# Attention by pairs of heads: scores in two row tiles, weights divided by their sums only in the output, keys tiled from the first meta token

## The chip, the core and the metric

The kernel runs on one core of a Trainium2 chip. TensorE (PE) multiplies matrices out of the on-chip memory SBUF into the accumulators in PSUM; PEld is its loading of the stationary operand. VectorE (DVE), ScalarE (ACT) and GpSimd (POOL) do elementwise work, and SyncE (SP) issues most of the DMAs. Every engine works through its own list of instructions in the order written. The metric is the time of one execution in microseconds, as the median of several runs.

## The reference, cut to what matters

Sixteen learned meta tokens go ahead of 512 tokens of width 1024. Layer 0 is an attention with a forget gate, layer 1 a gated recurrence, and each is followed by a mixture of 32 experts. The change is in layer 0's attention, with 16 heads of width 64:

```
h = concatenate([meta, x], axis=1)                 # 16 + 512 = 528 places
q, k = rms_norm per head (both with gains);  v;  log_f = log_sigmoid(f_logit + b_f)
cum = cumsum(log_f, axis=1)
s = einsum('bhqd,bhkd->bhqk', qi, kh) * scale + cum_q - cum_k
p = softmax(where(key_pos <= q_pos, s, -1e30), axis=-1)
o = einsum('bhqk,bhkd->bhqd', p, vh)
h = h + o @ w_out
```

All of it is float32.

## The kernel before

`fox` first projects tokens to q, k and v, half a matrix at a time (`chunk`), then calls `attend`. The projections split every float32 operand in a rounded part (`hi`) and its remainder (`lo`) and add three products. The query tokens lie in four tiles of 128 (`NT = 4`); the meta tokens are kept apart: `vm` holds the values of the 16 meta places and `v[:, j]` those of token tile j. Query tile i sees n = 16 + 128(i+1) keys: 144, 272, 400 and 528.

`attend` walks over the 16 heads. For a head,

- `key_bias` loads -cum of the keys, the same row on all 128 partitions, by four DMAs into one of four buffers `bias`, and POOL adds the causal mask to the four diagonal blocks;
- `scores` multiplies q and k. A head has 64 rows, head a = 0 of a pair on partitions 0 to 63 and a = 1 on 64 to 127. Each of the four blocks is three products of hi and lo (the first pair of heads: one product in float32). Then DVE adds bias to the scores, writes them over the bias and takes the row maximum in one instruction per block (line 703), and forms the exponent's offset `nb`;
- `soften` is ACT's exponential in place with the row sum `sm`, four instructions;
- `normalise` is DVE's multiplication of the weights by 1/`sm`, four instructions (line 724);
- `turn` transposes the weights on PE, 14 blocks (first 16 meta keys of each query tile, then 128 keys at a time), through two PSUM buffers `ptp`, each copied out by ACT or DVE to `PTm` and `PT`;
- `mix`, once per pair, multiplies the transposed weights with the values into `po`, the two heads side by side in two column tiles of 64, and `K.a.put` splits `po` into `ahi` and `alo` for the output projection.

The order is written by hand in the loop at the end of `attend`: the turn of head t-2, the softmax of head t-1 and the mix of an older pair are slipped between the four score blocks of head t, so that PE always has something else to do. `meta_scores` and `meta_turn` do the 16 meta queries of all heads. After the attention, `out_project` begins with ACT's split of a weight (`whi`, line 278), and opens the room for the experts' weights, which are then streamed from HBM.

Of the kernel before, what the change touches and what calls it, by code (L numbers as in the profile page):

```python
# [20 lines left out]
D = 1024  # L21
# [141 lines left out]
class Normed:  # L163
# [3 lines left out]
    def __init__(self, K, src, gain, pool, wk, ps, ptag, rs=None):  # L167

        self.K, self.src, self.wk, self.ps, self.ptag, self.rs = K, src, wk, ps, ptag, rs
        self.gb = gain[:, :, None]  # L170
        self.xs = {}
        self.hi = pool.tile([128, KJ, S], FR, name="xhi")
        self.lo = pool.tile([128, KJ, S], FR, name="xlo")

        self.m = pool.tile([128, KJ, 2 * M], FT, name="xm")
        K.nc.gpsimd.memset(self.m, 0.0)

    def tokens(self, i, j):
        cs = slice(128 * i, 128 * i + 128)
        return self.hi[:, j, cs], self.lo[:, j, cs]  # L180
# [31 lines left out]
    def turn(self, i, xs):  # L212
# [3 lines left out]
        for j0 in range(0, KJ, 4):  # L216
# [4 lines left out]
            if i == NT:  # L221
                nc.vector.tensor_tensor(self.m[:, j0:j0 + 4, :M], p[:, :, :r], g, op=OP.mult)
                continue
# [3 lines left out]
        cs = slice(128 * i, 128 * i + 128)  # L227
        for js, t in ts:
            nc.scalar.activation(self.hi[:, js, cs], t, AF.Copy)  # L229
        for js, t in ts:  # L230
            nc.vector.tensor_tensor(self.lo[:, js, cs], t, self.hi[:, js, cs].bitcast(FT), op=OP.subtract)  # L231

# [79 lines left out]
def row_terms(x, W, i, late=False):  # L312

    xs = [x.tokens(i, j) for j in range(KJ)]
# [12 lines left out]
def project(K, x, W, i, p, between, late):  # L327

    ts = row_terms(x, W, i, late)
# [36 lines left out]
def fox(K):  # L366
# [3 lines left out]
    with tc.tile_pool(name="ax", bufs=1, reuse_waits="tile") as per:  # L370
# [3 lines left out]
        vm = per.tile([M, D], FT, name="vm")  # L374
# [11 lines left out]
        with tc.tile_pool(name="ap", bufs=1, reuse_waits="tile") as mid, \  # L386
# [8 lines left out]
            def load(i):  # L395
                if i == NT:

                    nc.sync.dma_start(vm, K.meta_tokens)
                    loaded[i] = vm, M
                    return  # L400
# [3 lines left out]
            x = Normed(K, loaded.pop, gain, mid, nw, ps, "tr")  # L404
# [34 lines left out]
            def meta_done(mr, kind, half):  # L439
                if kind == "v":  # L440
                    mr.sum(vm[:, 512 * half:512 * half + 512])
                    return
# [5 lines left out]
            def meta_product(n):  # L448
                return MetaRows(K, x.m[:, :, :M], ps.tile([128, 512], FT, name="pm", tag="pm"), n)

            def chunk(kind, half, nxt):
# [3 lines left out]
                for i in range(NT):  # L455
# [9 lines left out]
                    project(K, x, W2, i, p, between, early)  # L465
                    if i == 0 and early:
                        mr = meta_product(2 * KJ)
# [8 lines left out]
                    if nxt and mr is None and not turns:  # L476
                        mr = meta_product(KJ)
# [83 lines left out]
        attend(K, qT, kT, v, vm, cq)  # L561


def forget_gate(K, x, wf, mid, ps, later, cq):
# [10 lines left out]
    def logits():  # L575
        p = ps.tile([128, 512], FT, name="pf", tag="pm")
        ts = []
        for j in range(KJ):
            ts += parts((wh[:, j], wl[:, j]), (x.hi[:, j], x.lo[:, j]))
# [44 lines left out]
def attend(K, qT, kT, v, vm, cq):  # L624
    nc, tc = K.nc, K.tc
    with tc.tile_pool(name="at", bufs=1, reuse_waits="tile") as mid, \
            tc.tile_pool(name="au", bufs=3, reuse_waits="tile") as wk, \
            tc.tile_pool(name="av", bufs=1, space=PSUM, reuse_waits="tile") as ps:
        B = K.B + [mid.tile([128, TOT], FT, name=f"bias{n}") for n in range(2, 4)]
        bias, PT, QK = {}, {}, {}  # L630

        def prepare(hd):
            bias[hd] = B[hd % 4]
            key_bias(K, hd, B[hd % 4])

# [28 lines left out]
        def split(hp):  # L664

            QK[hp] = []
            for n, src in (("q", qT[:, hp, M:]), ("k", kT[:, hp])):
                hi, lo = [wk.tile([128, src.shape[1]], FR, name=n + m, bufs=2) for m in ("hi", "lo")]
# [4 lines left out]
        def scores(hd):  # L673

            a, hp = hd % 2, hd // 2
            r = slice(64 * a, 64 * a + 64)

            qk = [(q[r], k[r]) for q, k in (parts(*QK[hp]) if hp else [(qT[:, 0, M:], kT[:, 0])])]
            b = bias[hd]
            mx = wk.tile([128, NT], FT, name="mx")  # L680
            nb = wk.tile([128, NT], FT, name="nb")
            todo = []
            for i in range(NT):
                n = M + 128 * (i + 1)
                qi = slice(128 * i, 128 * i + 128)
                bi = b[:, OFF[i]:OFF[i] + n]
                if i == 0:
                    pb = ps.tile([128, 512], FT, name="s0", tag="s0")
                if i < 2:
                    p = pb[:, 144 * i:144 * i + n]  # L690
                    accumulate(nc, p, [(q[:, qi], k[:, :n]) for q, k in qk])
                elif i == 2:
                    p = ps.tile([128, 512], FT, name="s2", tag="s2")[:, :n]
                    accumulate(nc, p, [(q[:, qi], k[:, :n]) for q, k in qk])
                else:
                    p = ps.tile([128, 2, 512], FT, name="s3", tag="s3")[:, :, :n // 2]
                    for u in range(2):
                        accumulate(nc, p[:, u], [(q[:, qi], k[:, n // 2 * u:n // 2 * (u + 1)]) for q, k in qk])
                    bi = bi.rearrange("q (u c) -> q u c", u=2)
                todo.append((p, bi))  # L700
                yield
            for i, (p, bi) in enumerate(todo):
                nc.vector.tensor_tensor_reduce(bi, p, bi, 1.0, NEG, op0=OP.add, op1=OP.max, accum_out=mx[:, i:i + 1])
            cqh = cq[:, :NT, hd]
            nc.vector.tensor_tensor(mx, mx, cqh, op=OP.add)
            nc.vector.tensor_tensor(nb, cqh, mx, op=OP.subtract)
            held[hd] = nb
            if a == 0 and hp + 1 < NH // 2:
                split(hp + 1)

        def soften(hd, nb):
            b = bias[hd]
            sm = wk.tile([128, NT], FT, name="sm")
            for i in range(NT):
                bi = b[:, OFF[i]:OFF[i] + M + 128 * (i + 1)]
                nc.scalar.activation(bi, bi, AF.Exp, bias=nb[:, i:i + 1], accum_out=sm[:, i:i + 1])
            return sm

        def normalise(hd, sm):
            b = bias[hd]  # L720
            nc.vector.reciprocal(sm, sm)
            for i in range(NT):
                bi = b[:, OFF[i]:OFF[i] + M + 128 * (i + 1)]
                nc.vector.tensor_scalar(bi, bi, sm[:, i:i + 1], None, op0=OP.mult)

        def turn(hd):

            b = bias.pop(hd)
            pt = wk.tile([128, 1280], FT, name="PT", bufs=4)
            ptm = wk.tile([M, S], FT, name="PTm", bufs=4)  # L730
            PT[hd] = (pt, ptm)
            for j in range(-1, NT):
                p = ps.tile([128, 512], FT, name="ptp", tag="pt", bufs=2)
                for i in range(max(j, 0), NT):
                    o = OFF[i] + (M + 128 * j if j >= 0 else 0)
                    n = 128 if j >= 0 else M
                    nc.tensor.transpose(p[:n, 128 * i:128 * i + 128], b[:, o:o + n], K.ident)  # L737
                c = 128 * max(j, 0)
                if j < 0:
                    nc.scalar.activation(ptm, p[:M], AF.Copy)  # L740
                elif j % 2:
                    nc.vector.tensor_copy(pt[:, POFF[j]:POFF[j] + S - c], p[:, c:])
# [1295 lines left out]
```

## Time and profile before

| | us |
|---|---|
| time, median of 3 runs (1782.38 to 1784.61) | 1783.42 |
| time of the profiled execution | 1778.16 |
| its span in the profile | 1776.2 |
| PE busy | 1621.1 |
| DVE busy | 773.2 |
| ACT busy | 411.7 |

Busy times are shares of the whole span. Matmuls are pipelined, so that one matmul's duration holds some latency, and what one costs in a stream is read from the start of one to the start of the next. The attention is about 116 us of the span, from 207 to 323 us.

### The profile page before, as it was taken

To read this page: it belongs to the slowest core of one execution; us is meant where nothing else is said; L and a number is where in the kernel's file an instruction comes from. 1 tells how busy PE (TensorE), PEld (TensorE's weight loads), DVE (VectorE), ACT (ScalarE), POOL (GpSimd) and SP (SyncE) were. 2 spreads that over 40 slices of the span, in tenths; PEclk is the share of its full clock that TensorE was granted. 3 is DMA by queue.
4 is the path that set the end of the run, shared out by engine and by line. 5 is a ranking of instruction groups with operands and counts; after the bars stand their busy time and mean duration, and the time that the engine had idled before them with its cause. 6 is when DMAs were issued, how large, how long until landed. Compare 5 with 4: busy or idle time off the path is not lost.

```text
span 1776.2 us, 23560 instructions
## 1 busy us (share of the span) xinstructions
PE 1621.1 (91%) x9397; PEld 881.2 (50%) x9397; DVE 773.2 (44%) x1834; ACT 411.7 (23%) x867; POOL 241.7 (14%) x205
## 2 busy tenths in 40 slices
PE   5998999986999999999979989989779999999997
PEld 3666766553344443433346667767533433333333
DVE  5664388353234342333461545665513333232334
ACT  5433266341001000000043323334401000000000
POOL 1412344100000000000032222313000000000000
PEclk9999899996999999999989999999889999999999
DMA  4212554448999999999911211114689999999995
GB/s 169 77 63 80 137 105 81 167 150 324 419 419 419 419 419 419 420 419 419 376 59 39 94 48 49 54 50 184 252 329 419 419 419 419 419 419 419 420 420 213
DMA packets 103558, 472.73 MB, mean 266 GB/s; under 512 B 16224, under 2 KB 34704, under 8 KB 54800
## 3 DMA queue, kind: packets, MB, share of 16 engines
q1 hardware_dynamic: 97248, 458.12, 65.8%
q0 software_dynamic: 5008, 8.76, 1.5%
q10 hardware_dynamic: 1184, 4.26, 0.6%
q8 instruction: 76, 1.25, 0.3%
q14 instruction: 42, 0.34, 0.1%
HBM read 472.97 MB, written 6.39 MB: 270 GB/s over the span
## 4 chain that ended last, share of the span: by engine, by line
PE 48%; DMA 35%; DVE 10%; ACT 4%; issue 1%; POOL 0%; ACTq 0%; DVEq 0%; SPq 0%; POOLq 0%
DMA w<-in_moe_w_up_dram 23%; PE pp L888 12%; DMA w<-in_moe_w_down_dram 11%; PE pa L1610 10%; PE pp L331 5%; PE py L1610 4%; PE pc L304 2%; PE s L304 2%; PE ptp L737 2%; PE pm L348 1%; PE po L761 1%; DVE Q L1066 1%; ACT xs L210 1%; PE pt L1591 1%; PE po L304 1%
## 5 line engine op out<-in xcount | busy, mean ns | idle before, releaser
L1610 PE MATMUL pa<-w,hm 128*64 128x512 f32 x1024 | 237.0, 600 | 16.9 <-DMA w<-in_moe_w_up_dram 16.9
L1610 PE MATMUL py<-w,hT 128*64 128x512 f32 x1024 | 244.6, 597 | 0.6 <-DMA w<-in_moe_w_down_dram 0.6
L1610 PE MATMUL pa<-w,xT 128*64 128x512 f32 x1024 | 234.5, 598 | 8.8 <-DMA w<-in_moe_w_up_dram 8.8
L286 POOL TENSOR_TENSOR wlo<-w,whi 128x2048 fp32r<-128x2048 f32 (+1 forms) x27 | 120.9, 4480 | 384.9 <-ACT whi L278 367.7
L1661 DVE TENSOR_TENSOR h<-pc,h 128x512 f32<-128x512 f32 x256 | 159.1, 682 | 21.3 <-PE pc L304 21.3
L1610 PEld LDWEIGHTS pa<-w,hm 128*64 128x64 f32 x1024 | 75.9, 138 | 169.3 <-issue 130.7
L1610 PEld LDWEIGHTS pa<-w,xT 128*64 128x64 f32 x1024 | 78.8, 137 | 156.4 <-issue 130.7
L1610 PEld LDWEIGHTS py<-w,hT 128*64 128x64 f32 x1024 | 73.7, 136 | 154.5 <-issue 137.8
L1596 DVE TENSOR_TENSOR hm<-pt,mg 128x512 f32<-128x512 f32 x32 | 22.1, 691 | 288.9 <-PE pt L1591 288.9
L1408 POOL DMA_INDIRECT xg<-xd,row x32 | 32.1, 1003 | 850.1 <-PE pt L1591 698.2
L1596 DVE TENSOR_TENSOR xT<-pt,mg 128x512 f32<-128x512 f32 x32 | 22.1, 691 | 284.7 <-PE pt L1591 284.7
L304 PE MATMUL pc<-yhi,OT 128*128 128x512 f32 (+1 forms) x288 | 127.4, 442 | 3.6 <-DVE OT L1644 2.9
L1625 ACT ACTIVATE sg<-pa 128x512 f32<-128x512 f32 x32 | 19.1, 597 | 463.3 <-PE pa L1610 463.3
L304 PE MATMUL pc<-ylo,OT 128*128 128x512 f32 (+1 forms) x288 | 114.8, 399 | 1.1 <-DVE ylo L1651 0.8
L1638 ACT ACTIVATE hT<-pth 128x512 f32<-128x512 f32 x32 | 19.2, 599 | 331.8 <-PE pth L1636 331.8
L331 PE MATMUL pp<-whi,xlo 128*128 128x512 f32 x192 | 80.2, 417 | 2.5 <-DVE xlo L231 2.5
L331 PE MATMUL pp<-whi,xhi 128*128 128x512 f32 x192 | 79.6, 415 | 2.1 <-ACT xhi L229 2.1
L304 PEld LDWEIGHTS pc<-yhi,OT 128*128 128x128 f32 (+1 forms) x288 | 52.9, 184 | 40.8 <-DVE h L1661 24.8
L888 PE MATMUL pp<-xhi,whi 128*128 128x512 f32 x168 | 71.9, 428 | 0.0
L888 PE MATMUL pp<-xlo,whi 128*128 128x512 f32 x168 | 67.9, 404 | 0.0
L278 ACT ACTIVATE whi<-w 128x2048 fp32r<-128x2048 f32 x32 | 61.1, 1917 | 0.0
L1650 ACT ACTIVATE yhi<-py,slot 128x512 fp32r<-128x512 f32 x64 | 42.2, 685 | 73.2 <-PE pc L304 46.7
(396 smaller groups left out, 2426.8 us busy)
## 6 DMA issues: line engine op xcount, KB each, us to landing
w<-in_moe_w_up_dram SPq DMA_DIRECT2D x256, 1024.0 KB, 19.9
w<-in_moe_w_down_dram SPq DMA_DIRECT2D x124, 1024.0 KB, 20.5
w<-in_hg_w_in_dram SPq DMA_DIRECT2D x16, 1024.0 KB, 5.3
w<-in_fox_w_in_dram SPq DMA_DIRECT2D x12, 1024.0 KB, 5.3
bias<-ncum SPq DMA_DIRECT2D x16, 264.0 KB, 4.1
w<-in_fox_w_out_dram SPq DMA_DIRECT2D x4, 1024.0 KB, 5.1
xd<-xn ACTq DMA_DIRECT2D x8, 512.0 KB, 4.9
w<-in_moe_w_down_dram SPq DMA_DIRECT2D x8, 512.0 KB, 16.8
```

The source lines that it names most:

```text
L278: nc.scalar.activation(hi, raw, AF.Copy)
L286: e.tensor_tensor(lo[:, js], raw[:, js], hi[:, js].bitcast(FT), op=OP.subtract)
L304: nc.tensor.matmul(p, a, b, start=(n == 0), stop=(n == len(terms) - 1))
L331: K.nc.tensor.matmul(p, a, b, start=(n == 0), stop=(n == len(ts) - 1))
L737: nc.tensor.transpose(p[:n, 128 * i:128 * i + 128], b[:, o:o + n], K.ident)
L888: nc.tensor.matmul(p, a, b, start=(m == 0), stop=(m == len(terms) - 1))
L1408: K.nc.gpsimd.indirect_dma_start(x, None, K.xd[self.layer], bass.IndirectOffsetOnAxis(ap=row, axis=0), bounds_check=K.xd[self.layer].shape ...
L1596: nc.vector.tensor_tensor(xT[:, js], p[:, :, :n], gain[:, js, None].to_broadcast([128, 4, n]), op=OP.mult)
L1610: nc.tensor.matmul(p[c][64 * a:64 * a + 64], x[:, j, 64 * a:64 * a + 64], w[a][c], start=(j == 0), stop=(j == nj - 1), skip_group_check=Tr ...
L1638: nc.scalar.activation(hT[:, :, :n], pt[:, :, :n], AF.Copy)
L1650: nc.scalar.activation(hi[:n], py[:n], AF.Copy, scale=g)
L1661: nc.vector.tensor_tensor(h[:, cs], p[:r], h[:, cs], op=OP.add)
```

## The change

It changes five things in layer 0's attention.

1. Values are projected for places and not for tokens: `v[:, 0]` now begins with the 16 meta places, and `vl` holds the last 16 places. For this the normalised tokens lie behind the meta tokens in one array (`lead`).
2. Keys are tiled from the first meta place, so that tile j holds places 128j to 128j+127, and each query tile has one further edge of 16 keys, which only its last 16 queries see. The turn copies four small blocks (`PTe`, 16 keys by 16 queries) where it copied 16 keys by 512 queries (`PTm`), and `mix` has eight products of 16 columns for a pair where it had two of 512.
3. `scores` does a pair of heads at a time, the two heads' matmuls in turn, each into a PSUM bank of its own. The 528 keys are two blocks of 264.
4. `normalise` is gone. The weights are turned undivided; 1/`sm` of a pair is spread over 64 partitions per head by eight small matmuls with the identity (`pr`), copied by ACT (`on`), and multiplied to `po` by DVE on the way out.
5. The loop runs over 8 pairs and two steps more: scores of pair t and mix of pair t-2 in pieces by turns, then the whole turn of pair t-1, then the exponentials of pair t. There are five bias buffers, and the double buffering of small tiles goes from 3 to 2.

```diff
-    def __init__(self, K, src, gain, pool, wk, ps, ptag, rs=None):
+    def __init__(self, K, src, gain, pool, wk, ps, ptag, rs=None, lead=0):
...
-        self.hi = pool.tile([128, KJ, S], FR, name="xhi")
-        self.lo = pool.tile([128, KJ, S], FR, name="xlo")
+        self.hi = pool.tile([128, KJ, lead + S], FR, name="xhi")
+        self.lo = pool.tile([128, KJ, lead + S], FR, name="xlo")
...
+        def scores(hp):
...
+            for n, blocks in enumerate((((0, 0, 0, 144), (1, 144, 0, 272)), ((2, 0, 0, 400),), ((3, 0, 0, 264),),
+                                        ((3, 0, 264, 264),))):
+                p = ps.tile([128, 2, 512], FT, name="s", tag="s", bufs=2)
+                for i, c, k0, w in blocks:
+                    for t, (q, k) in enumerate(qk):
+                        for a in range(2):
+                            r = slice(64 * a, 64 * a + 64)
+                            nc.tensor.matmul(p[:, a, c:c + w], q[r, 128 * i:128 * i + 128], k[r, k0:k0 + w],
+                                             start=(t == 0), stop=(t == len(qk) - 1))
+                for a in range(2):
...
+                        nc.vector.tensor_tensor_reduce(bi, p[:, a, c:c + w], bi, 1.0, NEG, op0=OP.add, op1=OP.max,
+                                                       accum_out=mx[:, a, m:m + 1])
+                yield
...
-        def normalise(hd, sm):
-            b = bias[hd]
-            nc.vector.reciprocal(sm, sm)
-            for i in range(NT):
-                bi = b[:, OFF[i]:OFF[i] + M + 128 * (i + 1)]
-                nc.vector.tensor_scalar(bi, bi, sm[:, i:i + 1], None, op0=OP.mult)
...
+                    if e:
+                        nc.vector.tensor_copy(pte, p[:M].rearrange("k (i q) -> k i q", i=NT)[:, :, 128 - M:])
+                        continue
...
+            nc.vector.reciprocal(rr, sums.pop(hp))
+            pr = ps.tile([128, 512], FT, name="pr", tag="pt", bufs=2)
...
+                    nc.tensor.matmul(pr[64 * a:64 * a + 64, 128 * i:128 * i + 128],
+                                     rr[:, a, i:i + 1].to_broadcast([128, 64]), K.ident, start=True, stop=True,
+                                     skip_group_check=True, tile_position=(0, 64 * a))
+            on = wk.tile([128, 512], FT, name="on")
+            nc.scalar.activation(on, pr, AF.Copy)
...
+            nc.vector.tensor_tensor(on, po, on, op=OP.mult)
+            K.a.put(hp, on)
...
+        for t in range(NP + 2):
+            sc = scores(t) if t < NP else iter(())
+            tu = turn(t - 1) if 0 <= t - 1 < NP else iter(())
+            mi = mix(t - 2) if t >= 2 else iter(())
+            if t + 1 < NP:
+                prepare(2 * t + 2)
+            for _ in range(4):
                 next(sc, None)
+                next(mi, None)
+            for n in range(8):
+                next(tu, None)
+                if n == 3 and t + 1 < NP:
+                    prepare(2 * t + 3)
             run(tu)
...
             run(sc)
...
+            if t + 2 < NP:
+                split(t + 2)
+            if t == 0:
                 meta_scores()
...
+            if t == 1:
                 meta_turn()
```

On PE, in the middle of the attention before, one head's list is this, from its last score block to the next head's first (line 304: scores, 737: transposes, 757 and 761: mix):

```order
L304 MATMUL s_2116<-khi,qhi 128x264
L304 MATMUL s_2116<-khi,qlo 128x264
L304 MATMUL s_2116<-klo,qhi 128x264
L737 MATMUL ptp<-ident,bias_85 16x128 x4
L737 MATMUL ptp<-ident,bias_85 128x128 x4
L757 MATMUL po<-PTm,vm 64x512 x2
L737 MATMUL ptp<-ident,bias_85 128x128 x3
L761 MATMUL po<-PT,v 64x512 x2
L737 MATMUL ptp<-ident,bias_85 128x128 x2
L304 MATMUL s_2178<-khi,qhi 128x144
```

In the change the same place, the end of one step and the start of the next, reads like this on PE (line 703: scores, 740: transposes, 756: the spread sums, 772: mix):

```order
L772 MATMUL po<-PTe,v 64x16 x6
L772 MATMUL po<-PTe,vl 64x16 x2
L772 MATMUL pom<-pTm,v 64x16 x2
L703 MATMUL s<-khi,qhi 128x264 x2
L703 MATMUL s<-khi,qlo 128x264 x2
L703 MATMUL s<-klo,qhi 128x264 x2
L740 MATMUL ptp<-ident,bias_1682 16x128 x4
L740 MATMUL ptp<-ident,bias_1682 128x128 x10
L740 MATMUL ptp<-ident,bias_85 16x128 x4
L740 MATMUL ptp<-ident,bias_85 128x128 x10
L756 MATMUL pr<-ident,rr 64x128 x8
L703 MATMUL s<-khi,qhi 128x144 x2
```

The 28 transposes of a pair now stand in one piece, with no score block and no mix between them.

On DVE before, the list of one head around its softmax is this (line 703: bias and maximum, 724: the division by the sum, 742: copies of the turn, 250: the split of the mix):

```order
L703 ISA bias_1674,mx<-s_2200,bias_1674 128x528
L703 ISA mx 128x1
L705 TENSOR_TENSOR mx<-mx,cq 128x4
L706 TENSOR_TENSOR nb<-cq,mx 128x4
L721 RECIPROCAL sm<-sm 128x4
L724 TENSOR_SCALAR bias_1673<-bias_1673,sm 128x144
L724 TENSOR_SCALAR bias_1673<-bias_1673,sm 128x272
L724 TENSOR_SCALAR bias_1673<-bias_1673,sm 128x400
L724 TENSOR_SCALAR bias_1673<-bias_1673,sm 128x528
L742 COPY PT<-ptp 128x384
L250 TENSOR_TENSOR alo_1661<-po,ahi_1660 128x256
```

In the change DVE's list reads like this between the mix of an older pair and the turn (line 786: the product with 1/`sm`, 261: the split, 710: the last score block, 742 and 746: copies of the turn):

```order
L786 TENSOR_TENSOR on<-po,on 128x512
L261 TENSOR_TENSOR alo_1668<-on,ahi_1667 128x256
L261 TENSOR_TENSOR alo_1670<-on,ahi_1669 128x256
L710 ISA bias_86,mx<-s,bias_86 128x264
L710 ISA mx 128x1
L710 ISA bias_1680,mx<-s,bias_1680 128x264
L710 ISA mx 128x1
L742 COPY PTe<-ptp 16x64
L746 COPY PT<-ptp 128x128
L746 COPY PT<-ptp 128x384
L742 COPY PTe<-ptp 16x64
L746 COPY PT<-ptp 128x128
```

The four divisions of a head are gone; the product, the split and the last score block now stand in front of the first copy of the turn.

## Rows read from the trace of the kernel before

**Rows 1.** Busy time by stage: window, length, PE, PEld, DVE, ACT, POOL, clock, DMA share, GB/s.
```profile
207.00:323.00 116.00, 110.06 (x703) 71.08 (x705) 90.68 (x310) 65.13 (x201) 48.01 (x73) 0.93 0.47 90
563.00:880.00 317.00, 306.45 (x1337) 124.64 (x1336) 112.61 (x174) 26.48 (x43) 7.95 (x8) 1.00 1.01 418
```
**Rows 2.** Chain that ended last, one pair of heads: start, us, what.
```profile
256.32 0.91 PE s L304 x6
...
257.49 1.47 PE s L304 x9
258.95 0.97 PE ptp L737 x8
259.93 1.00 PE po L757 x4
...
266.39 0.80 PE po L761 x4
...
268.47 0.22 PE pom L768 x4
...
269.06 0.90 PE s L304 x6
```
**Rows 3.** DVE in order of time: score blocks of one head, and its four divisions.
```profile
264.32 0.29 DVE L703 CUSTOM_DVE_ANT_0 bias<-s,bias 128x144 f32<-128x144 f32 x1
...
264.54 0.43 DVE L703 CUSTOM_DVE_ANT_0 bias<-s,bias 128x272 f32<-128x272 f32 x1
...
264.90 0.56 DVE L703 CUSTOM_DVE_ANT_0 bias<-s,bias 128x400 f32<-128x400 f32 x1
...
266.92 1.31 DVE L724 TENSOR_SCALAR bias<-bias,sm 128x144 f32<-128x144 f32 x4
```
**Rows 4.** PE in order of time, near the start of the attention.
```profile
217.53 1.87 PE L737 MATMUL ptp<-ident,bias 128*16 128x128 f32 x8
...
220.09 0.60 PE L645 MATMUL pmm<-kT,qT 64*16 64x16 f32 x30 [0.53 <-ACT PT L744]
```
**Rows 5.** Busy time and clock of the microsecond of those small matmuls.
```profile
220.00:221.00 1.00, 0.60 (x30) 0.49 (x30) 0.31 (x2) 0.04 (x1) 1.00 (x2) 0.50 0.21 57
```
**Rows 6.** Costliest groups of the page: a product on DVE out of PSUM.
```profile
L1661 DVE TENSOR_TENSOR h<-pc,h 128x512 f32<-128x512 f32 x256 | 159.1, 682 | 21.3 <-PE pc L304 21.3
```
**Rows 7.** Groups by form, 207 to 324 us: busy us, mean ns of one.
```profile
L737 PE MATMUL ptp<-ident,bias 128*128 128x128 f32 x160 | 31.6, 304 | 1.1 <-ACT PTm L740 0.7 <-DVE bm L648 0.3
...
L744 ACT ACTIVATE PT<-ptp 128x512 f32<-128x512 f32 x16 | 9.2, 574 | 0.5 <-PE ptp L737 0.5
...
L742 DVE COPY PT<-ptp 128x384 f32<-128x384 f32 x16 | 8.8, 548 | 2.4 <-PE ptp L737 2.4
...
L250 DVE TENSOR_TENSOR alo<-po,ahi 128x256 fp32r<-128x256 f32 x16 | 6.8, 424 | 9.3 <-ACT ahi L249 9.2
...
L249 ACT ACTIVATE ahi<-po 128x256 fp32r<-128x256 f32 x16 | 6.1, 384 | 18.4 <-PE po L761 13.8 <-DVE alo L250 4.5
```
**Rows 8.** ACT in order of time: first and last exponential instruction of one head.
```profile
263.10 0.41 ACT L716 ACTIVATE bias<-bias,nb 128x144 f32<-128x144 f32 x1
...
265.25 0.19 ACT L716 ACTIVATION_READ_ACCUMULATOR bias<-bias,nb 128x1 f32 x1
```
**Rows 9.** DMA issues of the page: KB each, us to landing.
```profile
bias<-ncum SPq DMA_DIRECT2D x16, 264.0 KB, 4.1
```
**Rows 10.** ACT in order of time: the end of the attention.
```profile
323.30 5.53 ACT L278 ACTIVATE whi<-w 128x2048 fp32r<-128x2048 f32 x3
```
**Rows 11.** Windows of 2 us around a wait of PE in the projections.
```profile
110.00:112.00 2.00, 0.27 (x5) 0.22 (x4) 1.76 (x7) 0.00 (x0) 0.49 (x1) 1.00 0.19 28
...
114.00:116.00 2.00, 2.00 (x6) 1.51 (x6) 1.51 (x8) 0.74 (x3) 0.00 (x0) 0.50 0.47 178
116.00:118.00 2.00, 2.00 (x8) 1.58 (x7) 0.54 (x4) 0.14 (x1) 0.00 (x0) 0.70 0.00 0
```

More of the change, by code (lines that the diff above doesn't have):

```diff
@@ L309, in parts, with row_terms @@
     return [(a[0], b[0]), (a[1], b[0]), (a[0], b[1])]
-def row_terms(x, W, i, late=False):
-    xs = [x.tokens(i, j) for j in range(KJ)]
+def row_terms(x, W, i, late=False, places=False):
+    xs = [x.columns(128 * i, j) if places else x.tokens(i, j) for j in range(KJ)]
     ts = []
@@ L440, in meta_done @@
                 if kind == "v":
-                    mr.sum(vm[:, 512 * half:512 * half + 512])
+                    mr.sum(vl[:, 512 * half:512 * half + 512])
                     return
@@ L764, in mix @@
+            for j in range(NT):
+                for a in range(2):
+                    product(po[:, 128 * j:], j, PT[2 * hp + a][0][:, POFF[j]:POFF[j] + S - 128 * j], a, start=(j == 0))
+                if j % 2:
                     yield
+            for i in range(NT):
+                for a in range(2):
+                    product(po[:, 128 * i + 128 - M:128 * i + 128], i + 1, PT[2 * hp + a][1][:, i], a, stop=True)
             for a in range(2):
-                r = slice(64 * a, 64 * a + 64)
@@ L767, in mix @@
-                cs = slice(64 * (2 * hp + a), 64 * (2 * hp + a) + 64)
-                nc.tensor.matmul(pom[r], vm[:, cs], pTm[:, 2 * hp + a, :], start=True, stop=True, skip_group_check=True,
-                                 tile_position=(0, 64 * a))
-            K.a.put(hp, po)
-            nc.scalar.activation(K.a.m[:, hp], pom, AF.Copy)
-        for hd in range(2):
-            bias[hd] = B[hd]
-        held = {}
-        mixing = []
-        tu = iter(())
-        for t in range(NH + 4):
-            sc = scores(t) if t < NH else iter(())
-            if 4 <= t < NH + 4 and t % 2 == 0:
-                mixing.append(mix((t - 4) // 2))
-            mi = mixing[-1] if mixing else iter(())
-            for _ in range(2):
-                next(sc, None)
-            run(tu)
-            if 1 <= t < NH - 1:
-                prepare(t + 1)
-            for _ in range(2):
-                next(sc, None)
-            if 0 <= t - 1 < NH:
-                held[t - 1] = soften(t - 1, held[t - 1])
-            tu = turn(t - 2) if 0 <= t - 2 < NH else iter(())
-            for _ in range(2):
-                next(tu, None)
+                product(pom, 0, pTm[:, 2 * hp + a, :], a, start=True, stop=True)
```

192 lines of the change are left out of this document (85 added, 107 removed).

## The prediction

> **What bounds the kernel now.** I read the busy times by stage first. From 207 to 323 us, the attention, PE is busy 110 of 116 us, DVE 91 and the DMAs half of the time [rows 1]. The experts that follow are at 418 GB/s [rows 1], but their stream begins only when `out_project` opens room, so it starts later or earlier with the attention's end, and I count what the attention wins or loses one to one. Then I read the chain that ended last, for one pair of heads: it is PE alone, row after row, from 256.32 to 269.06, or 12.74 us a pair [rows 2]. PE's time in a pair: scores 2 x (0.91 + 1.47) = 4.76; mix 2 x 1.00 (meta keys, tile 0) + 2 x 0.80 (tile 1, tiles 2 and 3) + 0.22 = 3.82, where one row stands for two that take the same; the 28 transposes the rest, 4.16 [rows 2]. So before the change nothing is waited for: the hand-made order covers every answer of ACT and DVE with other work on PE. That is what to look for behind the change.
>
> **What it removes and adds.** Removed: DVE's divisions, 1.31 us a head [rows 3]. DVE isn't on the chain, so this alone gives nothing. Removed on PE: the two meta products of a pair, 1.00. Added on PE: eight products of 16 columns; the nearest row has two such in 0.22 [rows 2], so 0.88; and eight `pr` matmuls of 128 columns, a quarter of the columns of the pairs that take 1.00 for two, four pairs of them, so 1.0. The sum of these three is +0.9 us a pair.
>
> The scores are what PE can save: if the heads' matmuls overlap, 2.38 instead of 4.76 a pair. Before shows one place where matmuls on the two halves of the partitions alternate: 30 small records of 16 columns in 0.60 us at half clock [rows 4, 5]. Less some 0.2 of latency that is 14 ns each; a record of 512 columns takes 0.5 alone (four in 1.00, two by two), so 16 columns at half clock take 31. I take full overlap as the likelier. The Trainium skill, TensorEngine Tiling (Array Packing), Theoretical Speedup, gives up to 2x for such tiles; by it the scores are 2.38 too. Its section PSUM Bottleneck says that tiling speeds up TensorE and not the emptying of PSUM, which speaks against the change; the next part finds that in this kernel's rows.
>
> Added on DVE: a product of 128x512 for each pair, 0.68 [rows 6]; four score blocks of 264 for two of 528. Sums of single engines would say that all is well: PE 2.38 + 3.70 + 3.4 (28 transposes at 0.12, [rows 2]) + 1.0 = 10.5, DVE about 9. But the order decides. The whole turn now stands in one piece on PE, behind all scores and mixes, and DVE's list puts product, split and the last score block ahead of the turn's first copy. One step, from PE's first score matmul at 0:
>
> 1. PE to the end of the mix: first block 0.91; mix of tiles 0 and 1, 1.80; block of 400, 0.63 (its part by columns, 1200 of 2784, of the 1.47 for nine matmuls); mix of tiles 2 and 3, 0.80; half of 264, 0.42; edges 1.10 [rows 2]. That is 5.65. PE then does its last scores and two groups of transposes to 6.7, and has no third buffer `ptp`.
> 2. DVE waits for `po` (0.2 of latency, estimated from a transpose's 0.30 beside its 0.12 in a stream), product 0.68: 6.55. `ahi` on ACT 0.38, then two `alo` of 0.42, the second begun a little before the first has ended: 7.7 [rows 7]. The last block of both heads, 0.36 each (that is what 272 columns take from start to start [rows 3]): 8.4.
> 3. Only now the first copy, of `PTe`, about 0.2. The other eight tiles pass through two buffers; each costs its transposes (0.30 for one, 0.12 more for each further), a copy (0.55 to 0.57 for a wide one, about 0.3 to 0.4 for a narrow one) and, estimated, 0.1 of signals [rows 2, 7]. The longer buffer is 3, 1, edge, 2, 0 and the other 2, 0, 3, 1: DVE's last copy, of the second head's tile 1, ends at 12.7. The reciprocal 0.17, then `pr` 1.0: the next step starts at **13.9**.
>
> So a pair takes 13.9 instead of 12.74. ACT's eight exponentials (2.25 a head from 263.10 to the end of the last [rows 8]) run beside the scores and are done at 5.3, in time. The second bias of a pair can be loaded only when the first head of the turn before is out of its buffer, about 4 us before the step; it takes 4.1 at most to land [rows 9], a mask 0.5, and is read at 1.7. I cost that at nothing; the two are close, and where it is late, the first score block is late by as much, up to 1 us. The fifth buffer takes that risk from the pair's first head. SP has only bias loads in this stretch, and POOL's masks and `lo` parts keep their number, so nothing else queues behind a late one. Two small buffers in place of three cost nothing: each is used again two steps later.
>
> **Start and end.** The scores of pair 0 are emptied by DVE from 208.1 to 211.7 (3.5 us for two heads [rows 3]), offsets at 212.3, eight exponentials to 216.8. `meta_scores` now stands ahead of pair 1's scores on DVE and its exponential behind those eight on ACT: DVE waits for it from 215 to 217.2, ends it at 218.3, and empties pair 1 until 222.2. The turn of pair 0 then runs at half clock, where eight transposes take 1.87 instead of 0.97 [rows 2, 4]: to 231. The six steps with scores and turn take 6 x 13.9 = 83.4, plus 1.8 while the clock is still low: 316.2. The last turn waits for no score block: 11.25, to 327.4; the last mix 3.7, product and split 1.7: 332.9. Before, ACT starts `whi` at 323.30 [rows 10]. The sum is **+9.6 us**. The few extra operations of 16 columns in the projections I bound by 0 and 0.5 and take as nothing.
>
> On the profiled execution's 1778.16 this is 1787.8; the median of the runs is 5.3 above that execution, so I forecast **1793**.
>
> **The rivals.**
>
> *The clock falls in every turn (chance 0.18).* PE at 2.4 GHz stands still from 6.7 to 8.7 in a step and then does single transposes with waits. In the projections a stretch of two thin microseconds (0.27 busy from 110 to 112) was followed by half clock, 1.2 GHz, at 114 to 116 and partly to 118, while PE was busy throughout [rows 11]. Near the attention's start, too, half clock is granted while PE does such small work [rows 5]. For it: each step has such a stretch. Against: no stretch of the steady part before has one. Price by these rows: about 1.8 in the dense part, 1.2 in the transposes, 1.0 in `pr`, so 4 a step: 6 x 4 + 2 = 26 more, **1819**. The Trainium skill, TensorE: Matmul & The Clock Gate, HAM oscillation, describes the same harm from gaps between bursts; the trace agrees that a gap is followed by half clock.
>
> *The row tiles don't overlap (0.08).* Then the change does not do what it says. The scores ahead of the product take 0.91 + 0.63 + 0.42 = 1.96 more, a step 15.9: +11.8, and pair 0 +1.5: **1806**. The 14 ns speak against it, on small matmuls only.
>
> *Faster: the step takes what its fullest engine takes (0.20).* The place is between PE's last scores and the first copy of the turn. If `ptp` copies and `alo` come back sooner than I chain them, PE never waits and a step tends to PE's 10.5: 6 x 3.4 = 20 less, **1773**. DVE's list speaks against it: it is strictly in order. It decides at a step of 12.3, where start and end are paid for.
>
> *No change that can be told (0.12).* A step of 11.7 to 12.9, around **1783**. Three runs spread over 2.2 us; I take 0.2% (3.6 us) as what can be told from no change.
>
> **How the numbers follow.** The forecast, a step of 13.0 to 15.2 (late copies at one end, a late bias at the other) and so 1787 to 1801, has 0.42. Slower: 0.42 + 0.18 + 0.08 = 0.68; same 0.12; faster 0.20. For the range I go from 1771, which leaves out a third of the faster case, to 1821, which leaves out the part of the clock's case in which two steps' worth more is lost.
>
> **What would show it.** In the profile after: a chain in the attention that goes PE, DVE, ACT, DVE and then copy by copy through `ptp`, no longer PE alone; a PE wait of 1.5 to 2.5 us in each turn that DVE's copy to `PTe` ends; steps of about 14 us from `pr` to `pr`; 30 score matmuls of a pair in about 2.4 us; the division's 20 us gone from DVE; expert stages of unchanged length. I am wrong if the scores take 3 us or more, if PE's waits in the turn are under 0.5, or if the clock at 240 to 310 us is not full.

## The result, and the profile after

The changed kernel takes 1795.32 us (median of 4 runs, 1794.72 to 1796.45), the kernel before beside it 1783.60 (4 runs, 1782.38 to 1784.61). The ratio is 1.0067, its 95% interval 1.0049 to 1.0084, or 8.7 to 15.0 us more. Forecast were 1793 and "slower" with 0.68. The profiled execution is one of these runs: 1795.00 us, with a span of 1793.2.

Busy time by stage of the changed kernel (window, length, PE, PEld, DVE, ACT, POOL, clock, DMA share, GB/s), beside [rows 1]:

```profile
208.30:339.00 130.70, 104.86 (x933) 68.83 (x932) 73.20 (x286) 63.31 (x194) 47.03 (x74) 0.84 0.41 81
563.00:880.00 317.00, 308.40 (x1354) 124.65 (x1355) 109.71 (x170) 26.50 (x43) 8.79 (x9) 0.99 1.01 419
```

The attention has less to do and takes longer: PE 104.9 us of work where it had 110.1, DVE 73 where it had 91, in 130.7 us where it took 116. PE stands still for 26 us in it, and it ran at a mean granted clock of 0.84 (0.93 before). The experts are DMA-bound as before. ACT's first `whi`, at 323.30 in [rows 10], is now here:

```profile
339.02 5.51 ACT L289 ACTIVATE whi<-w 128x2048 fp32r<-128x2048 f32 x3
```

One step of the changed kernel, PE in order of time (start, us, operation, in brackets the idle time before it and what ended it), beside [rows 2]. The chain that ended last can't be followed back beyond 438.92 in this profile, so that the attention is read from the engines themselves:

```profile
246.55 0.34 PE L703 MATMUL s<-khi,qhi 64*128 64x144 f32 x2
...
247.47 1.73 PE L772 MATMUL po<-PT,v 128*64 128x512 f32 x8
249.12 0.45 PE L703 MATMUL s<-khi,qhi 64*128 64x400 f32 x2
...
249.87 0.87 PE L772 MATMUL po<-PT,v 128*64 128x256 f32 x8
250.67 0.39 PE L703 MATMUL s<-khi,qhi 64*128 64x264 f32 x2
...
251.24 0.52 PE L772 MATMUL po<-PTe,v 16*64 16x16 f32 x12
...
251.92 0.39 PE L703 MATMUL s<-khi,qhi 64*128 64x264 f32 x2
...
252.48 0.71 PE L740 MATMUL ptp<-ident,bias 128*16 128x128 f32 x5
255.17 5.09 PE L740 MATMUL ptp<-ident,bias 128*128 128x128 f32 x23 [1.98 <-DVE PTe L742]
260.32 1.09 PE L756 MATMUL pr<-ident,rr 128*64 128x128 f32 x16
261.34 0.33 PE L703 MATMUL s<-khi,qhi 64*128 64x144 f32 x2
```

From first score matmul to first score matmul this is 14.8 us, where a pair took 12.74. All matmuls of scores and mix are done after 5.9; then PE does two groups of transposes and waits 1.98 for the copy to `PTe`. What DVE does meanwhile:

```profile
252.06 0.69 DVE L786 TENSOR_TENSOR on<-po,on 128x512 f32<-128x512 f32 x1
253.23 1.06 DVE L261 TENSOR_TENSOR alo<-on,ahi 128x256 fp32r<-128x256 f32 x2 [0.48 <-ACT ahi L260]
254.21 0.42 DVE L710 CUSTOM_DVE_ANT_0 bias<-s,bias 128x264 f32<-128x264 f32 x1
...
254.91 0.21 DVE L742 COPY PTe<-ptp 16x64 f32<-16x64 f32 x1
```

Product, split with a wait for ACT, and last score block, in this order, and only at 254.91, 8.36 after the step's start, the copy that PE waits for. Over all turns (groups of the page: busy, mean ns of one, idle time before and what ended it):

```profile
L740 PE MATMUL ptp<-ident,bias 128*128 128x128 f32 (+1 forms) x224 | 46.3, 364 | 16.4 <-DVE PTe L742 15.0 <-ACT PT L748 0.4
```

15.0 us of waits end with `PTe`'s copy. And the clock, in windows of 1 us (columns as above), which before was full in the steady part:

```profile
253.00:254.00 1.00, 0.19 (x2) 0.00 (x0) 0.77 (x2) 0.57 (x3) 1.00 (x3) 1.00 0.01 2
254.00:255.00 1.00, 0.00 (x0) 0.00 (x0) 1.00 (x6) 0.00 (x0) 1.00 (x3) 0.87 0.00 0
255.00:256.00 1.00, 0.83 (x4) 0.83 (x5) 0.32 (x2) 0.04 (x1) 0.43 (x2) 0.50 0.00 0
...
257.00:258.00 1.00, 1.00 (x7) 0.61 (x5) 0.10 (x1) 0.45 (x1) 0.00 (x0) 0.50 0.03 9
258.00:259.00 1.00, 0.91 (x6) 0.43 (x5) 0.50 (x2) 0.15 (x1) 0.00 (x0) 0.92 0.31 48
```

PE stands still from 253.2, and the granted clock falls to half (1.2 GHz) just before it goes on and stays there for 3.4 us, from about 254.74 to 258.16. In this step it is full again before `pr`. So this is the forecast's mechanism, and one that was held to be a rival besides.

### The profile page after: what moved, and what is told of

The parts are those of the page before. It is cut to its first block, busy times and chain, and to the rows that moved or that the text cites. A ratio compares the mean times of both kernels' runs of the same rounds, so it can differ in the third digit from the quotient of the medians.

```text
span 1793.2 us, 23961 instructions
## 1 busy us (share of the span) xinstructions
PE 1616.2 (90%) x9621; PEld 878.5 (49%) x9621; DVE 757.5 (42%) x1814; ACT 409.6 (23%) x861; POOL 240.3 (13%) x205
## 4 chain that ended last, share of the span: by engine, by line
DMA 34%; PE 33%; DVE 6%; ACT 2%; issue 1%; DVEq 0%; SPq 0%; POOLq 0%; ACTq 0%
DMA w<-in_moe_w_up_dram 22%; DMA w<-in_moe_w_down_dram 11%; PE pa L1616 10%; PE pp L894 10%; PE py L1616 5%; PE pc L315 3%; DVE Q L1072 1%; PE pt L1597 1%; PE po L315 1%; PE pm L360 1%; DVE KS L1075 1%; DVE h L1667 1%; PE lv L1019 1%; DMA xd<-xn 0%; ACT xs L216 0%
## 5 line engine op out<-in xcount | busy, mean ns | idle before, releaser
L740 PE MATMUL ptp<-ident,bias 128*128 128x128 f32 (+1 forms) x224 | 46.3, 364 | 16.4 <-DVE PTe L742 15.0
## 6 DMA issues: line engine op xcount, KB each, us to landing
bias<-ncum SPq DMA_DIRECT2D x16, 264.0 KB, 10.9
```

The source lines that it names most:

```text
L740: nc.tensor.transpose(p[:n, 128 * i:128 * i + 128], b[:, k:k + n], K.ident)
```

## The experiments

Theory after the result: a step is DVE's list up to the first copy (8.6 us), then copies through two buffers (4.4 at full clock, longer at half), then `pr` (1.0). Rivals: the clock is the larger part of the loss; the row tiles don't overlap; the buffers alone are at fault. "Attention" below is from the first score matmul to ACT's first `whi` in each profile, "step" the mean of five steps between starts of score blocks; times and ratios are against the kernel before on the same chip, whose medians lay between 1780.8 and 1783.6. The ratio need not be the quotient of the two medians; they lie up to 0.2% apart.

| kernel | time, us | ratio to before, 95% | attention | step |
|---|---|---|---|---|
| before, first profile | 1783.60 | | 116.2 | 12.74 |
| changed | 1795.32 | 1.0067 (1.0049 to 1.0084) | 130.7 | 15.03 |
| serial scores | 1795.57 | 1.0065 (1.0044 to 1.0085) | 130.9 | 15.14 |
| same rows | 1801.18 | 1.0095 (1.0064 to 1.0125) | 139.2 | 16.30 |
| fill of four | 1799.56 | 1.0089 (1.0067 to 1.0110) | 135.4 | 15.81 |
| fill of two | 1788.30 | 1.0032 (1.0009 to 1.0054) | 124.3 | 14.23 |
| three buffers | 1782.74 | 0.9985 (0.9962 to 1.0007) | 119.8 | 13.78 |
| meta early | 1794.03 | 1.0056 (1.0037 to 1.0075) | 128.8 | 14.99 |
| block late | 1791.52 | 1.0030 (1.0004 to 1.0057) | 130.4 | 15.14 |
| split late | 1776.45 | 0.9963 (0.9941 to 0.9986) | 112.1 | 12.50 |
| turn first | 1771.90 | 0.9934 (0.9913 to 0.9956) | 110.0 | 12.24 |
| turn first, meta early | 1770.09 | 0.9935 (0.9909 to 0.9961) | 110.6 | 12.22 |
| the same, three buffers | 1771.13 | 0.9932 (0.9910 to 0.9954) | 106.5 | 11.94 |

The kernels are timed to about 0.2%; differences of 1 or 2 us are read from attention and step. Attention and step come from one profiled execution each, and that execution isn't always near the median: it took 6.2 us more in three buffers (1788.90), 4.7 more in turn first with meta early (1774.77), 3.9 more in block late (1795.45) and 3.8 less in split late (1772.70). An execution's remaining time, from `whi` on, varies too: 1452.9 us in the first profile of before, 1449.7 in that of turn first, 1458.5 in that of three buffers.

### The kernel before, a second profile

> The kernel before once more, for a second profile. The profiled execution shown ahead of the prediction took 1778.16 us, 5.3 us under the median of its runs, and its attention ended (first `whi` on ACT) at 323.30. If the 5.3 us lie in the attention, the change cost less there than the 15.7 us between the two profiles (323.30 to 339.02); then this profile shows the attention's end near 327 at about 1783 us. If they lie elsewhere, the attention ends at 323.3 again.

One run, 1779.07 us, its attention from 205.67 to 324.39:

```profile
324.39 5.53 ACT L278 ACTIVATE whi<-w 128x2048 fp32r<-128x2048 f32 x3
```

Neither case: both profiles of the kernel before are of executions 4 to 5 us under the median, and this one's attention took 118.7 us and not 116.2. So the change lengthens the attention by 12.0 to 14.5 us, beside the 11.7 between the medians.

### Do the row tiles overlap?

```diff
-                    for t, (q, k) in enumerate(qk):
-                        for a in range(2):
+                    for a in range(2):
+                        for t, (q, k) in enumerate(qk):
```

> The changed kernel, but in each score block all matmuls of the first head stand before those of the second, no longer in turn. Theory (row tiles overlap when the heads alternate): a pair's 30 score matmuls, about 2.8 us of starts in the changed kernel (0.92 + 0.75 + 0.57 + 0.57), take nearly twice that; the three blocks ahead of the product grow by some 1.9 us, steps go from 14.9 to 16.8, and the time from 1795 to about 1808. Rival (the tiles do not overlap, the scores are cheap for another reason): no change, 1795.

No difference, 1.0065 beside 1.0067. By the expectation the theory falls, and the trace shows why it needn't (PE in order of time, one block):

```profile
258.90 0.34 PE L703 MATMUL s<-khi,qhi 64*128 64x144 f32 x2
259.07 0.28 PE L703 MATMUL s<-khi,qlo 64*128 64x144 f32 x2
259.19 0.28 PE L703 MATMUL s<-klo,qhi 64*128 64x144 f32 x2
...
259.82 1.73 PE L772 MATMUL po<-PT,v 128*64 128x512 f32 x8
```

In the list one head's three matmuls stand ahead of the other's; in the records the two heads still go side by side, and the block of twelve takes 0.92 us as before. So the order of the heads is no test. The next kernel takes the second tile away (both heads' scores are then made from the first head's rows, and the second head's own are left out):

```diff
-                            r = slice(64 * a, 64 * a + 64)
+                            r = slice(0, 64)
```

> The changed kernel, but the second head's score matmuls read the first head's half of the partitions, so that both heads use the same row tile (the second head's scores are then those of the first; nothing else differs). Theory (the two row tiles run at the same time, whatever the order of the heads in the list, which is why head after head changed nothing): without two tiles the 30 matmuls of a pair take 4.8 in place of 2.8 us; of the 2.0 some 1.6 lie ahead of the product, so steps go from 14.9 to 16.5, and seven pairs give 11 us: about 1806. Rival (no overlap; the scores got cheaper because their matmuls stand together): 1795.

The same twelve matmuls (start of the first to start of the mix), and the next three blocks:

```profile
266.26 0.44 PE L703 MATMUL s<-khi,qhi 64*128 64x144 f32 x2
...
267.88 1.73 PE L772 MATMUL po<-PT,v 128*64 128x512 f32 x8
269.53 0.63 PE L703 MATMUL s<-khi,qhi 64*128 64x400 f32 x2
...
270.83 0.87 PE L772 MATMUL po<-PT,v 128*64 128x256 f32 x8
```

1.62 and 1.30 in place of 0.92 and 0.75; with 0.92 and 0.94 for the blocks of 264 it is 4.78 a pair, what one head after the other took before (4.76, [rows 2]), against 2.80 (0.92 + 0.75 + 0.57 + 0.56) with two tiles. The overlap is real and worth 2.0 us of PE a pair. Of it 1.3 reach the step (16.30 against 15.03), less than the expected 1.6, because PE's wait for DVE shrinks from about 2 us to 1.3 to 1.5; the time, 1801, is 5 under what was expected.

### What does the clock cost?

```diff
+            if 2 <= t:
+                f = ps.tile([128, 2, 512], FT, name="fill", tag="s", bufs=2)
+                for n in range(4):
+                    nc.tensor.matmul(f[:, n % 2], K.ident, v[:, n % NT, :512], start=True, stop=True)
             for n in range(8):
                 next(tu, None)
```

> The changed kernel, with four extra f32 matmuls of 512 columns for each pair, into a free score buffer that nobody reads, between the last score block and the turn, where PE waits about 2 us for DVE's first copy. They add no needed work and fit into the wait (4 x 0.43 = 1.7). Theory (PE's stillness makes the granted clock fall from 1.0 to 0.5 at the turn's start, and that costs about 1 us a step, since the turn is bound by its copies): the clock stays at 1.0 in the turn, its second part goes from 5.1 to 5.8 us to about 4.2, seven turns give 6 to 9 us, about 1788. Rival, with the forecast's price of the clock (4 us a step): 25 us less, about 1770. If the clock falls all the same, or the fill delays the turn: 1795 to 1800.

```profile
253.31 3.70 PE L805 MATMUL fill<-v,ident 128*128 128x512 f32 x8
...
257.75 0.77 PE L740 MATMUL ptp<-ident,bias 128*128 128x128 f32 x5 [0.20 <-DVE PTe L742]
...
262.18 1.09 PE L756 MATMUL pr<-ident,rr 128*64 128x128 f32 x16 [0.38 <-DVE mx L713]
```

The fill was mis-sized: an f32 matmul is two records of 0.44 us each, so that four take 3.5 us, and PE goes on 10.4 us into the step (257.75 less 247.38) and not 8.6. But the clock stayed at 1.0, and from the first copy to `pr` the turn took 4.43 us, against 4.93 to 5.76 in the six turns of the changed kernel. With two matmuls, in the wait itself:

```diff
             for n in range(8):
                 next(tu, None)
+                if n == 0 and 2 <= t <= NP:
+                    f = ps.tile([128, 2, 512], FT, name="fill", tag="s", bufs=2)
+                    for u in range(2):
+                        nc.tensor.matmul(f[:, u], K.ident, v[:, u, :512], start=True, stop=True)
```

> As the kernel that filled the wait, but right-sized: two extra f32 matmuls of 512 columns (1.77 us by the 3.54 that four took), behind the turn's first two groups of transposes, where PE waits 1.95 to 2.2 us. Theory (the clock costs what the turn was longer at 0.5: 5.1 to 5.8 us against 4.4): steps of 13.9 to 14.1 as the forecast had them without the clock, whole time 6 to 9 us less, 1787 to 1790. Rival (4 us a step): 1767 to 1771. If the fill delays the first copy after all, or the clock falls behind it: 1793 to 1797.

Time 1788.3, in the theory's range. PE in one step of this kernel, then its window over the six steps (232 to 318 us):

```profile
259.59 0.33 PE L703 MATMUL s<-khi,qhi 64*128 64x144 f32 x2
...
268.25 0.76 PE L740 MATMUL ptp<-ident,bias 128*128 128x128 f32 x5 [0.31 <-DVE PTe L742]
...
272.68 1.09 PE L756 MATMUL pr<-ident,rr 128*64 128x128 f32 x16 [0.37 <-DVE mx L713]
273.70 0.34 PE L703 MATMUL s<-khi,qhi 64*128 64x144 f32 x2
```

The window:

```profile
232.00:318.00 86.00, 77.87 (x690) 48.24 (x688) 51.92 (x206) 47.41 (x147) 34.91 (x55) 1.00 0.46 84
```

The same window of the changed kernel:

```profile
232.00:318.00 86.00, 72.45 (x633) 47.33 (x631) 50.49 (x200) 45.18 (x141) 35.26 (x56) 0.87 0.46 86
```

With work that nobody needs, PE goes on where it did (8.66 into the step, 8.62 without the fill), the clock is full, and this step takes 14.1 (14.2 in the mean of five) in place of 15.0. The attention is 6.4 us shorter, the time 7.0. As far as two profiles can tell, that is the clock's whole price, 0.8 to 0.9 a turn and not the 4 that the rival was given: the six turns of the changed kernel take 5.28 in the mean, and 4.43 with the fill. The Trainium skill, TensorE: Matmul & The Clock Gate, A second HAM failure mode: psum-queue depth-cycling, tells of throughput lost to the clock between bursts when PE is briefly idle again and again; the two runs agree, with this small price.

### Which part of DVE's list?

All three parts moved (product behind the first copies, split and last score block behind the first head's third copy):

```diff
-            K.a.put(hp, on)
-            nc.scalar.activation(K.a.m[:, hp], pom, AF.Copy)
+            nc.scalar.activation(K.a.m[:, hp], pom, AF.Copy)
+            yield
...
+            yield
+            K.a.put(hp, on)
...
-            for _ in range(4):
+            for _ in range(3):
...
                 next(tu, None)
+                if n in (0, 2):
+                    next(mi, None)
+                if n == 2:
+                    next(sc, None)
...
+            run(mi)
             run(tu)
```

> The changed kernel with another order of the same operations: the turn begins as soon as the mix is done, and DVE's product of `po`, the split and the last score block stand between copies of the turn of the first head. Theory (DVE's list ahead of the first copy is what PE waits for): the wait of 2 us in each turn goes, first copy at about 6.0 in a step and not at 8.4, some of DVE's 2.3 us comes back between the copies, the clock stays at 1.0; steps of 12.0 to 12.8 in place of 14.9, about 1776 to 1781. Rival (DVE has as much to do as before and the turn waits for it later): 1791 to 1795.

1771.9 us, 11 under the kernel before, and better than the theory's range. One turn on PE:

```profile
250.75 0.77 PE L740 MATMUL ptp<-ident,bias 128*128 128x128 f32 x5 [0.20 <-DVE PTe L742]
...
254.05 0.77 PE L740 MATMUL ptp<-ident,bias 128*128 128x128 f32 x5 [0.36 <-DVE PTe L742]
...
255.66 1.09 PE L756 MATMUL pr<-ident,rr 128*64 128x128 f32 x16
```

The wait is 0.20, and the moved work comes back as waits of 0.2 to 0.6. The steps are 12.24, in the expected range. Then the split alone (`K.a.put` behind the third copy):

> The changed kernel with the split of the mix alone (two `ahi` on ACT, two `alo` on DVE) moved from ahead of the turn's first copy to behind the first head's third copy. Theory (the wait is the sum of what DVE does ahead of the first copy: 0.68 product, 1.5 for the split with its wait for ACT, 0.7 last block): the first copy comes 1.4 to 1.5 us earlier, PE's wait is about 0.5, so short that the clock stays at 1.0, and the split itself fits beside the turn: steps of 12.5 to 13.0, time 1780 to 1783. Rival (the split comes back in full between the copies, or the clock falls all the same): 1787 to 1792.

```profile
254.56 0.34 PE L703 MATMUL s<-khi,qhi 64*128 64x144 f32 x2
...
261.62 0.77 PE L740 MATMUL ptp<-ident,bias 128*128 128x128 f32 x5 [0.42 <-DVE PTe L742]
...
266.05 1.09 PE L756 MATMUL pr<-ident,rr 128*64 128x128 f32 x16 [0.37 <-DVE mx L713]
```

PE goes on 7.06 us into the step (8.62 before), its wait is 0.42, the clock over all steps is 1.00 (window 232 to 308), and from there to `pr` it takes 4.43 as with the fill. The steps are 12.50. So the split alone is worth 2.5 of the 15.0 us: 1.6 of list and about 0.85 of clock. The turn behind the wait is no longer for it, so the split comes back nowhere in the step. The last turn gains too, since PE's wait of 2.94 there, read below, is 0.22. At 1776.45 the time is under the expected one as well. And the last score block alone (its `next(sc)` behind the third copy):

> The changed kernel with the last score block alone (its matmuls and DVE's two additions) moved behind the first head's third copy. Theory, by the same sum: the first copy 0.7 earlier, but PE's 0.57 of matmuls no longer fill its wait, which stays near 2 us, so the clock falls in each turn as before; steps of 14.2 to 14.8, time 1789 to 1794. Rival (any shortening of DVE's list is enough): 1783 or less.

No gain in the profiled execution: step 15.14. PE's wait stays at 1.5 to 2.1 us, and the clock falls as before (0.86 from 232 to 316):

```profile
268.80 1.32 PE L740 MATMUL ptp<-ident,bias 128*128 128x128 f32 x5 [1.99 <-DVE PTe L742]
270.06 0.59 PE L703 MATMUL s<-khi,qhi 64*128 64x264 f32 x2
```

The copy comes earlier, but PE has lost the work that stood in the wait and does it later, inside the turn and here at half clock (0.59 where it is 0.39). That is a little more than the theory's 14.2 to 14.8. The time, 1791.5, fits the theory, though its interval overlaps with that of the changed kernel, and its profiled execution was 3.9 us over the median. The rival, that any shorter list is enough, is out: it asked for 1783 or less.

### The buffers

```diff
-tag="pt", bufs=2
+tag="pt", bufs=3
-            pom = ps.tile([128, M], FT, name="pom", tag="pm")
+            pom = ps.tile([128, M], FT, name="pom", tag="pt", bufs=3)
```

> The changed kernel with three buffers for the turn's transposes in place of two (the mix of the meta queries moves into the same ring, so that PSUM is as full as before). Theory (a step is DVE's list ahead of the first copy, to 8.6, and then the ping-pong through two buffers, 4.4 at full clock and 5.1 to 5.8 as granted): the wait ahead of the first copy stays near 2 us, since DVE is late and not a buffer, but the part behind it shrinks to about 4.0; steps of 13.5 to 14.2, time 1784 to 1790. Rival (the buffers were the whole of it, the wait shrinks too): 1776 or less. Rival (DVE's list and clock alone): 1793 to 1796.

Time 1782.7, no difference from before, some 13 us under the changed kernel and a little under the theory's range. The waits of a step in which the clock fell:

```profile
250.88 0.44 PE L740 MATMUL ptp<-ident,bias 128*128 128x128 f32 x2 [0.43 <-ACT am L788]
251.85 0.86 PE L740 MATMUL ptp<-ident,bias 128*128 128x128 f32 x3 [0.53 <-ACT PT L748]
253.54 4.10 PE L740 MATMUL ptp<-ident,bias 128*128 128x128 f32 x18 [0.84 <-DVE PTe L742]
```

The one wait of 2 us becomes three that add up to 1.8, with transposes between them; the first of them is for the meta mix (`pom`), which now shares the ring. In some steps the clock falls all the same (15.1 and 15.4 us), in the others it stays full (12.6 to 13.3). So the third buffer acts on both terms, the way through the buffers and the clock, and the theory was wrong that PE would wait near 2 us in one piece. It isn't the whole: with two buffers and the split moved the step is 12.50. The profiled execution was the longest of the twelve, and in how many steps of the others the clock fell isn't known.

### The start

```diff
+            if t == 0:
+                meta_scores()
             run(sc)
...
-            if t == 0:
-                meta_scores()
```

> The changed kernel with the softmax of the meta queries ahead of pair 0's maxima and exponentials, and not behind them. Theory (in the start DVE waits 2.2 us for the meta exponential, which stands behind eight others on ACT, and PE waits 7.06 us for DVE there): pair 1's score blocks are emptied some 3 us earlier, PE's wait there is about 4 us, and everything behind moves by about 3: 1792. Rival (the first turn then waits for pair 0's exponentials, or the start is covered): 1795.

```profile
217.13 0.41 DVE L669 TENSOR_REDUCE mxm<-bm 16x16 f32<-16x256 f32 x1 [0.48 <-ACT bm L668]
...
221.80 0.44 DVE L710 CUSTOM_DVE_ANT_0 bias<-s,bias 128x272 f32<-128x272 f32 x1 [1.07 <-POOL bias L636]
```

DVE's wait for the meta exponential, 2.58 us in the changed kernel, is 0.48. But the casts of `split` now stand behind it, and pair 1's blocks wait 1.07 for a mask on POOL. From the first score matmul to the first `pr` it is 20.7 us in place of 21.8: 1.1 won of the 3 expected, and 1.3 in the time, which this measurement cannot tell from nothing.

### Toward a version that beats both

Turn first and meta early together, then with three buffers (the diffs above):

> The order with the turn ahead of product, split and last score block, with the meta softmax moved ahead as in the run before. Theory: the steps stay at 12.2 us, the start gives the 1.1 us that it gave alone; 1769 to 1772. Rival (the start is covered in this order, or its wait for a mask grows): 1771 to 1774, no difference from the turn-first order alone.

> The same, and three buffers for the transposes. Theory (what is left of PE's waits in a step of 12.2, some 1.1 to 1.3 us in five pieces of 0.2 to 0.5, is the latency of copies through two buffers): steps of 11.2 to 11.7, 4 to 7 us less than with two: 1763 to 1768. Rival (DVE, with some 10 us of work in a step, is now as full as PE, and copies come no sooner): 1769 to 1772.

1770.1 and 1771.1: both 0.65 to 0.68% under the kernel before, not to be told from turn first alone (1771.9). The first expected 1769 to 1772 and got it, but the attention shows no gain from the meta part (110.6 beside 110.0), so the profile speaks for the rival, and the time can't decide. The third buffer, in this order, brings the step from 12.22 to 11.94, not to 11.2 to 11.7, and the attention from 110.6 to 106.5. Between these two profiled executions 3.5 of the 4 us are in the whole time (1774.77 and 1771.31), but the first of them was 4.7 over its median, and the medians show no gain. The profile of turn first alone took 1771.31 too, with an attention of 110.0: beside it the 3.5 us are lost again behind `whi` (1453.1 in place of 1449.7). What takes them isn't settled; the granted clock from 362 to 420 us was 0.69, beside 0.72 with two buffers and 0.75 in turn first alone.

## Why the prediction was right, and where it was not

**The bound, and PE's work.** The sum of PE alone (10.5) said a gain, the order said a loss, and the order decided. In the one step shown, PE is through the mix 5.37 us after the start (forecast 5.65): the mix with its small products is shorter, 3.13 for 3.70, the scores longer, 2.80 for 2.38, under the 3 that would have refuted the overlap. Same rows gave the 2.0 us a pair that the overlap saves.

**DVE's list.** Both `alo` were forecast to end at 7.7, the last block at 8.4, the first copy right behind; measured, by the start of what follows, 7.66 and 8.36. PE's wait, 1.68 to 2.21 us in the six steps, was forecast at 1.5 to 2.5. This step of the sum carried the prediction, and split late shows it as a cause: without the split ahead of the copy, PE goes on 1.6 us earlier.

**From the first copy to `pr`.** Forecast from 8.6 to 12.9. With the clock full (fill of two) it took from 8.66 to 13.09, so that the ping-pong through two buffers is right within 0.2 us, and the steps, 14.2 in the mean, within 0.3 of 13.9.

**The clock: the step that failed.** The forecast took a full clock in the steady part and gave "the clock falls in every turn" as a rival, with 0.18 and 4 us a step. It does fall, in each of the six steps (mean 0.87 from 232 to 318), so by the prediction's own sign this point was wrong. The price was wrong too: it is half for 3.4 us of a step (6.8 in one of the six), but full again before the dense part, at the latest 0.3 us into `pr`, and the turn is bound by copies and not by PE, so that half clock costs 0.8 to 0.9 a turn, 6.4 us in all. The forecast had 0, the rival 26.

**The start and the end.** The first step with a mix began at 231.63 (forecast 231), but two errors cancel in that: DVE's wait for the meta exponential ended at 219.26 (forecast 217.2), and the clock was full again from 227.4, so that the turn of pair 0 did not run at half clock throughout. The last turn took 13.2 us, from the mix ahead of it to the last mix (forecast 11.25):

```profile
326.61 0.71 ACT L260 ACTIVATE ahi<-on 128x256 fp32r<-128x256 f32 x2
327.98 5.62 PE L740 MATMUL ptp<-ident,bias 128*128 128x128 f32 x23 [2.94 <-DVE PTe L742]
```

DVE's product is done at 325.09, but `ahi` stands on ACT behind the eight exponentials of the last pair, some 1.5 us of PE's 2.94, and the clock falls to half again. The forecast counted only that no score block stands in the way. The last mix and product took 4.5 (forecast 5.4).

**The sum.** Forecast was `whi` at 332.9; it came at 339.02. The 6.1 us between: 0.6 start, 4.5 in the six steps, 1.95 in the last turn, -0.95 at the end. That the time was nearer than that is luck: with the 15.7 us that lie between the two profiles the same sum would have given 1799, but the profiled execution of before was 5.4 under its median, and between the medians it is 11.7. The 9.6 of the sum lie inside the interval, 8.7 to 15.0.

**What was costed at nothing.** The largest of a head's four bias loads takes 10.9 us to land (median; 4.1 before, [rows 9]), and DVE's first block of a step waits for its mask:

```profile
247.68 0.31 DVE L710 CUSTOM_DVE_ANT_0 bias<-s,bias 128x144 f32<-128x144 f32 x1 [1.04 <-POOL bias L636]
...
249.98 0.57 DVE L710 CUSTOM_DVE_ANT_0 bias<-s,bias 128x400 f32<-128x400 f32 x1 [1.04 <-PE s L703]
```

It starts some 0.6 us after its matmuls are through, but DVE then waits 1.04 for PE's next block, so that in this step nothing comes of it. This was argued from the trace and not tried; nor was the loss of the divisions, forecast to be without effect, tried alone. The forecast's 2.25 us for a head's exponentials reads 2.34 in [rows 8]; they were done in time all the same.

## What to carry to other kernels

Where a hand-made order hides every answer behind other work, a change that saves work on each engine can still lose: add up what stands in the strictly ordered list of the helping engine ahead of the first thing that the bound engine needs, and move from there what nobody waits for (here the split of an older pair, needed only by the next stage, worth 2.5 of 15.0 us a step). If a standing still lowers the clock, price that by what bounds the stretch behind it; where that is copies, half the clock costs little. Keep the work that fills a wait where the wait is.

## What the runs showed of the hardware

Matmuls on two halves of the rows ran side by side whether the list alternates between them or has three of one ahead of three of the other: 0.92 us for twelve either way, 1.62 on one half. An f32 matmul of 512 columns, left of 128 rows, is two records of 0.44 us at full clock, twice what I had reckoned for the fill. In the changed kernel each of PE's waits for `PTe` in the turns (1.7 to 2.9 us) came with a fall to half clock for 3.4 us, twice for 6.8, although PE was then busy. Waits of 0.4 us, or the same wait filled with matmuls that nobody reads, left the clock at 1.0. But with three buffers it fell in two steps, near 251.9 and 292.9, behind waits of only 0.4 and 0.5 us, and in the other steps, with like waits, it stayed full: the length of a wait alone doesn't settle it.
